# A decoder layer on one core: the gates' weight sums made in place on VectorE, and the down projections' sums read from scratch

## The chip, the cores and the metric

The kernel runs on one core of a Trainium2 chip. The metric is device time in microseconds. Three timed runs of the kernel before gave a median of 2127.15 us (2127.11 to 2127.19).

## The reference

One layer of a hybrid decoder, for 16 learned and 256 given positions (only the 256 are returned), model width 2048. All arrays are float32.

```python
u = rms_norm(h, g1);  h = h + 0.5 * (silu(u @ w_gate) * (u @ w_up)) @ w_down      # first FFN, width 5632
u = rms_norm(h, g2);  z = u @ w_in                                               # q k v, indexer, conv, two gates
y_attn = sparse_attention(q, k, v, indexer top 64) @ w_attn_branch
y_conv = (b * causal_conv3(c * xc)) @ w_conv_branch
merged = sigmoid(ga) * y_attn + sigmoid(gc) * y_conv
h = h + merged @ w_out
u = rms_norm(h, g3);  h = h + 0.5 * (silu(u @ w2_gate) * (u @ w2_up)) @ w2_down  # second FFN
```

## The kernel before

TensorE multiplies in float32r, which keeps only part of a float32 number. So every weight block is split on the chip into a rounded part (whi, ScalarE, L250) and the rest (wlo, VectorE, L251), and one product is three matmuls: activation-high by whi, activation-high by wlo, activation-low by whi (L641 to L643, and L430 to L432 in the earlier stages).

The program is one stream of weights. `Stream.loads` lists the transfers, in order, into a ring in on-chip memory of 12 slots of 128x512 elements; `Stream.subs` lists the units that are split, at most 1024 columns each. SyncE's queue issues the loads (L216), and a load is issued when the units that had its slots are split. A unit is split into one of four buffers of whi and wlo, and three units ahead of the one that TensorE works on (`AHEAD`). Each call of `Stream.next` that opens a unit issues, in this order, the steps due early, the split three units on, the loads that then fit, and the steps due late. So the order of each engine's instructions is fixed when the program is built.

The stages in order of time: first FFN (to about 800 us), input projections with the attention, the convolution (to 1090), the gates with the two branch products (1090 to 1343), the output projection, the second FFN (from 1434).

In the gates and in the second FFN the products go by pairs: two blocks of 128 input rows by two blocks of 512 columns. A plain pair (kind "C") takes eight products with 128 tokens each and four weight blocks in two units. The others save one product, as in Winograd's form of Strassen's method: seven products, with seven weight blocks, four of which are sums or differences of the weights (the signs lie in the token side), in four units of 2, 2, 2 and 1 blocks. The seven results are put together afterwards on VectorE (`recombine`, L720 to L723). Two ways of making the weight sums exist:

- Kind "P": `Stream.prepare` does it long ahead. GpSimd's queue fetches the 1 MB of four blocks (L178), VectorE makes four adds of 512 columns (L182), GpSimd's queue stores the result to a scratch tensor in DRAM (L185), and the stream later loads it from there. Most of these run in the first FFN; `LATE` says how many run in the input projections and how many beside the convolution. The 15 seven-product pairs of the gates (3 in the first group of 512 columns, 4 in each of the other three) and the 52 of the second FFN's gate and up projections are of this kind.
- Kind "D", in the down projections of the second FFN: shortly before use, one load on SyncE's queue (L163) and one accumulating transfer on GpSimd's queue (L164) make two of the sums, and VectorE the other two (L228, L229).

The down projection runs in three parts, over four, four and three groups of 512 hidden columns, each in two halves of 1024 output columns. A half of a long part has eight pairs, three of kind D; a half of the short part has six, two of kind D. The token side's sums for them are made in `turn_mid`.

A group of gates has eight pairs, then 8 units of branch weights, multiplied with the attention's and the convolution's results (`pbr`), then `merge` (six VectorE steps, L1242 and L1244), which is issued at the start of the next group.

## Time and profile before

| what | value |
|---|---|
| time, median of three runs | 2127.15 us |
| the profiled execution's own time | 2127.65 us |
| its span, first to last instruction | 2125.8 us |
| TensorE busy | 2109.4 us |
| VectorE busy | 1638.3 us |
| ScalarE busy | 1125.2 us |
| granted TensorE clock | 1.000 |

Rows of instructions give line, engine, operation, output and inputs, shapes and a count, then busy time and the mean of one in ns, then the idle time before them and what ended it. A row of the timeline begins with its start and its length in us, and ends in brackets with the idle time of the engine before it and what ended that. Waits give in total, times, longest. Rows by stage give, per engine, busy us and the number of instructions, then the granted clock, the DMA engines' share and GB/s. PE is TensorE's matmuls, PEld its weight loads, DVE VectorE, ACT ScalarE, POOL GpSimd, SP SyncE; q behind one is its queue. In rows of transfers the last number is the median time from issue to landing.

### The profile page before, as it was taken

The numbers are of one execution on the slowest core, as the hardware profiler recorded it, in microseconds if no ns is written. First come the engines' busy times: TensorE is split into PE (matmuls) and PEld (weight loads), VectorE is DVE, ScalarE is ACT, GpSimd is POOL, SyncE is SP. The second block draws the span as 40 slices with busy tenths as digits, with TensorE's granted clock in tenths as the row PEclk, the third lists the DMA queues.
The fourth block names the chain that finished last, engine by engine and source line by source line (L and its number), as shares of the span: only waits on it lengthen the run. The fifth ranks groups of instructions, "written<-read, shape, count | busy, mean of one in ns | idle before, by whom it ended". The sixth has DMA issues, their size and how long they took to land.

```text
span 2125.8 us, 33282 instructions
## 1 busy us (share of the span) xinstructions
PE 2109.4 (99%) x12973; PEld 1902.1 (89%) x12973; DVE 1638.3 (77%) x2150; ACT 1125.2 (53%) x1455; POOL 122.8 (6%) x196
## 2 busy tenths in 40 slices
PE   8999999999999999999999999999999999999999
PEld 8999999999999999888988888888888888888887
DVE  7777766677777766788777777687898889888887
ACT  5444433344444445555455566467675566656664
POOL 2000000000000110000000000010000000000000
PEclk9999999999999999999999999999999999999999
DMA  7798899988999967855577777567888888789884
GB/s 284 289 349 337 335 352 338 357 338 336 350 343 350 341 220 272 306 199 211 219 262 240 246 268 252 177 211 249 301 320 269 259 318 316 259 256 302 304 273 149
DMA packets 126302, 603.60 MB, mean 284 GB/s; under 512 B 14048, under 2 KB 14176, under 8 KB 85312
## 3 DMA queue, kind: packets, MB, share of 16 engines
q1 hardware_dynamic: 104256, 451.98, 59.7%
q0 software_dynamic: 21744, 149.33, 19.8%
q8 instruction: 101, 1.65, 0.3%
q14 instruction: 57, 0.47, 0.1%
q10 hardware_dynamic: 144, 0.17, 0.0%
HBM read 529.07 MB, written 72.35 MB: 283 GB/s over the span
## 4 chain that ended last, share of the span: by engine, by line
PE 96%; DVE 2%; ACT 1%; DMA 1%; POOL 0%; issue 0%; SPq 0%; DVEq 0%
PE q L641 13%; PE q L642 13%; PE q L643 13%; PE pd L430 4%; PE pd L432 4%; PE pd L431 4%; PE pu L432 4%; PE pg L432 4%; PE pg L431 4%; PE pu L431 4%; PE pg L430 4%; PE pu L430 4%; PE po L445 3%; PE po L447 1%; PE pbr L641 1%; PE pbr L643 1%
## 5 line engine op out<-in xcount | busy, mean ns | idle before, releaser
L251 DVE TENSOR_TENSOR wlo<-raw,whi 128x1024 fp32r<-128x1024 f32 (+1 forms) x887 | 1018.8, 1165 | 437.2 <-ACT whi L250 423.6
L250 ACT ACTIVATE whi<-raw 128x1024 fp32r<-128x1024 f32 (+1 forms) x887 | 888.0, 1011 | 881.6 <-PE q L643 220.2
L641 PE MATMUL q<-whi,act 128*128 128x512 f32 x713 | 278.8, 391 | 0.0
L643 PE MATMUL q<-whi,act 128*128 128x512 f32 x713 | 277.6, 389 | 0.0
L642 PE MATMUL q<-wlo,act 128*128 128x512 f32 x713 | 277.5, 389 | 0.0
L430 PE MATMUL pd<-mid,whi 128*128 128x272 f32 x704 | 201.8, 287 | 0.0
L432 PE MATMUL pd<-mid,wlo 128*128 128x272 f32 x704 | 201.8, 287 | 0.0
L431 PE MATMUL pd<-mid,whi 128*128 128x272 f32 x704 | 201.8, 287 | 0.0
L430 PE MATMUL pg<-act,whi 128*128 128x272 f32 x672 | 192.8, 287 | 0.0
L432 PE MATMUL pg<-act,wlo 128*128 128x272 f32 x672 | 192.6, 287 | 0.0
L431 PE MATMUL pg<-act,whi 128*128 128x272 f32 x672 | 192.6, 287 | 0.0
L430 PE MATMUL pu<-act,whi 128*128 128x272 f32 x672 | 192.6, 287 | 0.0
L432 PE MATMUL pu<-act,wlo 128*128 128x272 f32 x672 | 192.6, 287 | 0.0
L431 PE MATMUL pu<-act,whi 128*128 128x272 f32 x672 | 192.6, 287 | 0.0
L182 DVE TENSOR_TENSOR prep<-prep 128x512 f32<-128x512 f32 x268 | 183.2, 684 | 9.8 <-DMA prep<-in_w2p_dram 9.4
L643 PEld LDWEIGHTS q<-whi,act 128*128 128x128 f32 x713 | 133.9, 188 | 27.9
L642 PEld LDWEIGHTS q<-wlo,act 128*128 128x128 f32 x713 | 133.9, 188 | 27.2
L641 PEld LDWEIGHTS q<-whi,act 128*128 128x128 f32 x713 | 133.9, 188 | 27.2
L430 PEld LDWEIGHTS pd<-mid,whi 128*128 128x128 f32 x704 | 132.6, 188 | 0.0
L431 PEld LDWEIGHTS pd<-mid,whi 128*128 128x128 f32 x704 | 132.6, 188 | 0.0
L432 PEld LDWEIGHTS pd<-mid,wlo 128*128 128x128 f32 x704 | 132.6, 188 | 0.0
L431 PEld LDWEIGHTS pg<-act,whi 128*128 128x128 f32 x672 | 126.6, 188 | 0.0
(281 smaller groups left out, 3859.6 us busy)
## 6 DMA issues: line engine op xcount, KB each, us to landing
raw<-in_wgu_dram SPq DMA_DIRECT2D x87, 1024.0 KB, 7.2
raw<-in_w_dram SPq DMA_DIRECT2D x128, 512.0 KB, 5.7
prep<-in_w2p_dram POOLq DMA_DIRECT2D x52, 1024.0 KB, 9.0
s<-prep POOLq DMA_DIRECT2D x52, 1024.0 KB, 6.1
raw<-s SPq DMA_DIRECT2D x104, 512.0 KB, 5.9
raw<-in_wd_dram SPq DMA_DIRECT2D x44, 1024.0 KB, 6.7
raw<-in_w2p_dram SPq DMA_DIRECT2D x52, 512.0 KB, 6.2
raw<-in_wcv_dram SPq DMA_DIRECT2D x24, 1024.0 KB, 4.8
```

The source lines that it names most:

```text
L182: nc.vector.tensor_add(x[out], x[a], x[b])
L250: nc.scalar.activation(to[0], raw, AF.Copy)
L251: nc.vector.tensor_sub(to[1], raw, to[0].bitcast(F32))
L430: nc.tensor.matmul(ps, whi, xhi, start=first, stop=False)
L431: nc.tensor.matmul(ps, whi, xlo, start=False, stop=False)
L432: nc.tensor.matmul(ps, wlo, xhi, start=False, stop=last)
L445: nc.tensor.matmul(ps.rearrange("p (a t) -> p a t", a=2), whi, x(i), start=i == 0, stop=False)
L447: nc.tensor.matmul(ps[:, :SEQ], wlo, x(i)[:, 0, :], start=False, stop=i == total - 1)
L641: nc.tensor.matmul(ps, xhi, whi, start=n == 0, stop=False)
L642: nc.tensor.matmul(ps, xhi, wlo, start=False, stop=False)
L643: nc.tensor.matmul(ps, xlo, whi, start=False, stop=n == total - 1)
```

## The change

1. The gates' 15 seven-product pairs become kind "Q". Nothing is prepared for them: the raw weights of a pair are loaded into the ring, and `sum_ahead` makes the four sums on VectorE in the ring's own slots, at the step before the one that splits the pair's first unit. The number and size of the stream's loads there stay, and so do their places in the ring.
2. Kind "D" is gone, with its accumulating transfers. The down projections' seven-product pairs are of kind "P", and a half of a long part has four of them in place of three; a half of the short part keeps two.
3. So 72 pairs are prepared in place of 67. `LATE` moves one from beside the convolution to the input projections, and the steps of those beside the convolution start eight units later.
4. In the second FFN the ring grows by six slots in place of two; the room is that of the tiles that D used.
5. In the last half the last two results are finished one after the other (`apart`), where before their products alternated.
6. The token sums for `turn_mid` have a fourth place, and are made one step later.

```diff
-LATE = (7, 5)
+SUMS = ((1, 1, 0), (0, 0, 2), (2, 2, 1), (3, 3, 2))
+LATE = (8, 4)
...
-    return list(zip("CCCPPPCC", [0, 2, 4, 3, 5, 7, 6, 1]) if c == 0 else zip("CPPCPPCC", [0, 3, 5, 2, 7, 1, 4, 6]))
+    return list(zip("CCCQQQCC", [0, 2, 4, 3, 5, 7, 6, 1]) if c == 0 else zip("CQQCQQCC", [0, 3, 5, 2, 7, 1, 4, 6]))
...
-            ("CCDCDCDC", [(0, 2), (1, 2), (0, 0), (2, 2), (1, 0), (3, 0), (2, 0), (3, 2)]),
-            ("CDCDCDCC", [(0, 2), (0, 0), (1, 2), (1, 0), (2, 2), (2, 0), (3, 0), (3, 2)]),
+            ("CCPPCPPC", [(0, 2), (1, 2), (0, 0), (1, 0), (2, 2), (2, 0), (3, 0), (3, 2)]),
+            ("CPPCPPCC", [(0, 2), (0, 0), (1, 0), (1, 2), (2, 0), (3, 0), (2, 2), (3, 2)]),
...
-        self.loads += [(src[:, 2 * WIDE : 4 * WIDE], 2 * WIDE), (src[:, 4 * WIDE :], WIDE)]
-        self.added[g] = len(self.doubles)
-        self.doubles.append((g, src))
-        self.subs += [(g, "sa", 0, 2, WIDE), (g, "sb", 0, 2, WIDE), (g, "raw", 0, 2, WIDE), (g + 1, "raw", 0, 1, WIDE)]
+        src = ahead.pop(0)
+        g = len(self.subs)
+        self.add(src, 4, WIDE, False)
+        self.add(src[:, WIDE:], 3, WIDE, False)
+        self.subs[g] = (self.subs[g][0], "sums") + self.subs[g][2:]
...
-        self.ring += [(raw, i) for i in range(2)]
+        self.ring += [(raw, i) for i in range(6)]
...
         for g, kind, _, _, _ in self.subs[self.n_split : self.n_split + 2]:
-            if kind == "sa" and self.sum_pool and g not in self.summed:
+            if kind == "sums" and g not in self.summed:
                 self.load(g + 2)
                 self.summed.add(g)
-                one, last = self.raw[g], self.raw[g + 1]
-                sb = self.sum_pool.tile([P, 2 * WIDE], F32, name="sb", tag="sb")
-                add(sb[:, :WIDE], self.sums[g, "sa"][:, WIDE:], one[:, :WIDE])
-                add(sb[:, WIDE:], sb[:, :WIDE], last[:, :WIDE])
-                self.sums[g, "sb"] = sb
+                x = [self.raw[g + j // 2][:, j % 2 * WIDE : (j % 2 + 1) * WIDE] for j in range(4)]
+                for out, a, b in SUMS:
+                    self.nc.vector.tensor_add(x[out], x[a], x[b])
...
+        if apart:
+            w = [st.next(), st.next()]
+            for c, xs in ((c1, (b21, b11)), (c2, (b22, b12))):
+                for x, block in zip(xs, w):
+                    mac3(c, x, block)
+            return
...
-        st.prepare(lambda i: mp.tile([P, RAW], F32, name="prep", tag="tA"), LATE[1], 1, units2 + 6, units2 + 46)
+        st.prepare(lambda i: mp.tile([P, RAW], F32, name="prep", tag="tA"), LATE[1], 1, units2 + 14, units2 + 47)
```

Two places on VectorE show how the instructions move. The first is the third group of gates, from the end of `merge` on. `wlo<-raw,whi` is the split of a unit (1024 or 512 columns); before:

```order
L1244 TENSOR_TENSOR vm_13276<-va,vx 128x512
L1244 TENSOR_TENSOR vm_13277<-vv,ve 128x512
L251 TENSOR_TENSOR wlo<-raw,whi 128x1024 x2
L251 TENSOR_TENSOR wlo<-raw,whi 128x512
L251 TENSOR_TENSOR wlo<-raw,whi 128x1024 x3
L251 TENSOR_TENSOR wlo<-raw,whi 128x512
L251 TENSOR_TENSOR wlo<-raw,whi 128x1024 x5
L251 TENSOR_TENSOR wlo<-raw,whi 128x512
```

And now, where `raw<-raw` x4 is one in-place sum of a Q pair:

```order
L1220 TENSOR_TENSOR vm_12859<-va,vx 128x512
L1220 TENSOR_TENSOR vm_12860<-vv,ve 128x512
L228 TENSOR_TENSOR wlo<-raw,whi 128x1024 x2
L212 TENSOR_TENSOR raw<-raw 128x512 x4
L228 TENSOR_TENSOR wlo<-raw,whi 128x512
L228 TENSOR_TENSOR wlo<-raw,whi 128x1024 x3
L228 TENSOR_TENSOR wlo<-raw,whi 128x512
L228 TENSOR_TENSOR wlo<-raw,whi 128x1024
L212 TENSOR_TENSOR raw<-raw 128x512 x4
L228 TENSOR_TENSOR wlo<-raw,whi 128x1024 x4
L212 TENSOR_TENSOR raw<-raw 128x512 x4
L228 TENSOR_TENSOR wlo<-raw,whi 128x512
```

The second pair's sum stands ahead of the first pair's last unit; the third's stands ahead of the second unit of the plain pair between; the fourth's ahead of the third pair's last unit. The rest of the order is as before.

The second place is beside the convolution, where the attention's softmax begins (`soft`, `mx`, `sm`); `prep<-prep` is an add of a prepared pair. Before:

```order
L1152 SCALAR_TENSOR_TENSOR cy<-cx,small,cy 128x256 x2
L182 TENSOR_TENSOR prep<-prep 128x512
L251 TENSOR_TENSOR wlo<-raw,whi 128x1024
L453 TENSOR_TENSOR t<-pb,u 128x256
L1160 TENSOR_TENSOR cy<-t,cy 128x256
L467 TENSOR_TENSOR cs_10039<-cy,cs_10039 128x256
L1023 SCALAR_TENSOR_TENSOR soft<-psc,acc_8834 128x576
L1029 TENSOR_REDUCE mx<-soft 128x4
L1023 SCALAR_TENSOR_TENSOR soft<-psc,acc_8835 128x544
L1029 TENSOR_REDUCE mx<-soft 128x2
L182 TENSOR_TENSOR prep<-prep 128x512
L251 TENSOR_TENSOR wlo<-raw,whi 128x1024
```

And now:

```order
L1128 SCALAR_TENSOR_TENSOR cy<-cx,small,cy 128x256 x2
L228 TENSOR_TENSOR wlo<-raw,whi 128x1024
L425 TENSOR_TENSOR t<-pb,u 128x256
L1136 TENSOR_TENSOR cy<-t,cy 128x256
L439 TENSOR_TENSOR cs_10086<-cy,cs_10086 128x256
L999 SCALAR_TENSOR_TENSOR soft<-psc,acc_8874 128x576
L1005 TENSOR_REDUCE mx<-soft 128x4
L999 SCALAR_TENSOR_TENSOR soft<-psc,acc_8875 128x544
L1005 TENSOR_REDUCE mx<-soft 128x2
L228 TENSOR_TENSOR wlo<-raw,whi 128x1024
```

The first pair's adds are gone from this stretch, and the four pairs that stay come later.

## The prediction

> **What bounds the kernel now.** I read the page's head, the waits of TensorE, busy time by stage, and then the gates stage on the timeline.

> ```profile
> span 2125.8 us, 33282 instructions
> PE 2109.4 (99%) x12973; PEld 1902.1 (89%) x12973; DVE 1638.3 (77%) x2150; ACT 1125.2 (53%) x1455; POOL 122.8 (6%) x196
> PE start L430 <- ACT whi L250: 7.0, 1, 7.0
> PE psc L1017 <- DVE soft L1023: 1.0, 1, 1.0
> PE pcg L432 <- DVE wlo L251: 0.9, 2, 0.6
> PE q L641 <- DVE vx L1359: 0.7, 1, 0.7
> PE pqt L921 <- DVE zz L824: 0.3, 1, 0.3
> ...
> core 0: us, PE busy (x) PEld busy (x) DVE busy (x) ACT busy (x) POOL busy (x), PEclk, DMA share, GB/s
> 39.00:800.00 761.00, 761.00 (x6170) 760.81 (x6168) 540.35 (x715) 314.91 (x380) 66.85 (x119) 1.00 0.87 328
> 930.00:1090.00 160.00, 157.86 (x1129) 145.41 (x1128) 123.28 (x204) 82.17 (x159) 13.43 (x18) 1.00 0.61 218
> 1090.00:1343.00 253.00, 252.49 (x1123) 208.17 (x1122) 183.04 (x201) 146.88 (x168) 0.00 (x0) 1.00 0.73 247
> 1434.00:2100.00 666.00, 665.05 (x2993) 550.42 (x2992) 576.88 (x667) 427.86 (x498) 14.03 (x16) 1.00 0.84 283
> ```

> TensorE works 2109.4 of 2125.8 us, and what it waits between start and tail is under 4 us. So a gain can only come from fewer matmuls, and a loss from any place where VectorE stops keeping ahead. In the gates stage (1090 to 1343) VectorE has 183.0 us of work in 253, which looks like 70 us of room; in the second FFN (1434 to 2100) it is at 87% and TensorE still never starves. The question is whether the room in the gates lies where the new work falls.

> **The matmuls removed.** Each of the four long down halves turns one plain pair (eight products) into a seven-product pair: 4 products, 12 matmuls.

> ```profile
> 1199.78 0.39 PE L641 MATMUL pbr<-whi,ys 128*128 128x512 f32 x1
> ...
> 1200.46 0.39 PE L641 MATMUL pbr<-whi,cs 128*128 128x512 f32 x1
> ```

> Three starts in 0.68 us: a product costs 0.68, not three times the 0.39 that one record shows. So **-2.7 us**.

> **The second FFN's accumulating transfers.** GpSimd's sixteen leave, with two sums each on VectorE.

> ```profile
> L228 DVE TENSOR_TENSOR sb<-sd,raw 128x512 f32<-128x512 f32 x16 | 10.9, 682 | 0.0
> L229 DVE TENSOR_TENSOR sb<-sb,raw 128x512 f32<-128x512 f32 x16 | 11.1, 692 | 0.6
> sd<-in_w2d_dram POOLq DMA_DIRECT2D x16, 512.0 KB, 8.1
> ```

> 22 us of VectorE work and 8.1 us landings go, but TensorE waited only 0.7 us there (L1359), so at most that comes back; the other way, each of the four exchanged pairs is split in four units instead of two, well under the 22 us. I take 0 (-0.7 to +1). The ring, four slots larger than before in this stage, can hide more, but nothing is exposed.

> **The prepared sums.** 67 pairs were summed ahead, now 72: 60 instead of 55 in the first FFN, 8 instead of 7 in the projections, 4 instead of 5 beside the convolution.

> ```profile
> L182 DVE TENSOR_TENSOR prep<-prep 128x512 f32<-128x512 f32 x268 | 183.2, 684 | 9.8 <-DMA prep<-in_w2p_dram 9.4 <-DMA prep<-in_wgp_dram 0.3
> prep<-in_w2p_dram POOLq DMA_DIRECT2D x52, 1024.0 KB, 9.0
> s<-prep POOLq DMA_DIRECT2D x52, 1024.0 KB, 6.1
> 966.57 0.69 DVE L182 TENSOR_TENSOR prep<-prep 128x512 f32<-128x512 f32 x1
> ```

> In the first FFN that is 20 more adds (20 x 0.684 = 14 us, into 221 us of idle) and 10 more transfers of 1 MB on GpSimd's queue, 10.5 MB beside the 250 MB (761 us at 328 GB/s) that keep the DMA engines at 0.87: they go to about 0.91. I take 0 (0 to +2). Beside the convolution the pair taken away is the first, whose adds stood among the softmax steps; the wait of psc and one of pcg follow directly behind the one at 966.57. I take **-0.9** (-2 to 0).

> **The tail.**

> ```profile
> 2119.26 3.73 SPq L1402 DMA_DIRECT2D out_dram<-ht  x4
> 2121.26 1.37 DVE L1399 SCALAR_TENSOR_TENSOR ht<-q,ht 128x512 f32<-128x512 f32 x2 [1.35 <-PE q L643]
> ```

> The last half's last tile still ends with the last matmul; the tile before it is now finished one product (0.68) earlier, so two output transfers overlap less. **-0.3** (-0.7 to 0).

> **The gates: 15 in-place sums.** Each is four adds of 512 columns on one piece of the ring, each reading what the one before wrote. The nearest rows, a dependent add behind another and then an unrelated split:

> ```profile
> 1598.09 0.68 DVE L228 TENSOR_TENSOR sb<-sd,raw 128x512 f32<-128x512 f32 x1
> 1598.80 0.69 DVE L229 TENSOR_TENSOR sb<-sb,raw 128x512 f32<-128x512 f32 x1
> 1599.41 1.22 DVE L251 TENSOR_TENSOR wlo<-raw,whi 128x1024 fp32r<-128x1024 f32 x1
> ```

> A dependent add starts 0.71 after the one before, an unrelated instruction 0.61 after: a sum is 3 x 0.71 + 0.61 = 2.74 us. [...]

> Now the third group of gates (C Q Q C Q Q C C). I call a, b, c, d the four units of a seven-product pair (two weight blocks each, d one) and a, b the two of a C pair.

> ```profile
> 1215.42 0.39 PE L641 MATMUL q<-whi,act 128*128 128x512 f32 x1
> ...
> 1215.13 0.68 DVE L1242 TENSOR_TENSOR va<-pbr,va 128x512 f32<-128x512 f32 x1
> ...
> 1218.73 2.35 DVE L251 TENSOR_TENSOR wlo<-raw,whi 128x1024 fp32r<-128x1024 f32 x2
> 1221.72 0.69 DVE L251 TENSOR_TENSOR wlo<-raw,whi 128x512 fp32r<-128x512 f32 x1 [0.64 <-ACT whi L250]
> ...
> 1221.06 0.63 ACT L250 ACTIVATE whi<-raw 128x512 fp32r<-128x512 f32 x1 [1.66 <-PE q L643]
> ...
> 1228.76 1.06 ACT L250 ACTIVATE whi<-raw 128x1024 fp32r<-128x1024 f32 x1 [0.52 <-DMA raw<-in_wg_dram]
> 1230.01 1.07 ACT L250 ACTIVATE whi<-raw 128x1024 fp32r<-128x1024 f32 x1 [0.18 <-DMA raw<-sg]
> 1232.09 1.06 ACT L250 ACTIVATE whi<-raw 128x1024 fp32r<-128x1024 f32 x1 [1.01 <-DMA raw<-sg]
> ...
> 1224.77 1.69 SPq L216 DMA_DIRECT2D raw<-sg  x2
> ...
> raw<-in_wb_dram SPq DMA_DIRECT2D x32, 512.0 KB, 6.3
> raw<-sg SPq DMA_DIRECT2D x26, 512.0 KB, 4.7
> ```

> Three things stand in it. A unit costs VectorE 1.13 (2.35 for two, the last shown 1.22), a half one 0.61; so a Q pair is 3 x 1.13 + 0.61 + 2.74 = 6.7 us of VectorE for 7 x 0.68 = 4.76 of TensorE. ScalarE's rounding waits for TensorE to release one of four buffers ("<-PE q"), so splits run at most three units ahead: 4 us of a Q pair; VectorE cannot use its idle time of the branch products for later pairs. And the ring is already at its limit: the last rounding above (Q3a and Q3b are the two "sg" waits) waited 1.01 for a load issued by 1226.46 and landed at 1232.09, 5.6 us later. Its slot came free with the split of Q2b, and the sum of the third Q pair needs that same load, but stands one unit earlier on VectorE, with the split of Cb queued behind it and TensorE waiting for Cb.

> With the clock at 0 at 1215.42: the merge and Q1b, Q1c end at 5.7 as now. Sum 2 ends at 8.4, Q1d at 9.0, Q2a (rounded after its sum, 1.06) at 10.7. TensorE comes to Q2a at 10.2 and can do one matmul without the low part: it stops 0.3. Q2b is split at 11.9, Ca at 14.8. Sum 3 needs Q3b's load, issued at 12.0, landed at 17.4 (5.4 us, between the stage's median of 4.7 and this place's 5.6): it ends at 19.5, Cb's split at 20.7. TensorE wanted that at 18.2: **2.5**. Q3c is split at 24.1; sum 4 needs the load into Cb's slot, issued at 20.8 and landed at 25.5, ends at 27.6 and Q3d at 28.2, against 27.4: **0.8**. Q4a at 29.9 against 28.9: **1.0**. Behind that come the two C pairs, 10.9 us of TensorE for 4.5 of splits, and the backlog is gone. Together 4.6 us, in three groups 13.8. The first group (C C C Q Q Q C C) has no C between, but the token sums of one pair (1.7 us) fall in: the same reckoning stops at Q2c 0.3, Q2d 2.7 and Q3a 0.9, together 4. The gates: **+17.8 us**.

> Bounds: with every load there in time only work counts. VectorE then needs, from the merge through Q4a, 3.3 + 11 x 1.13 + 3 x 0.61 + 3 x 2.74 = 25.8 us and twice 0.5 where it waits for the rounding behind a sum: 26.8, against 5.44 + 4.76 + 4.76 + 5.44 + 4.76 + 0.23 = 25.4 at which TensorE wants it. [...] With landings of 7 us (the slowest kind of this stage, the branch weights, has 6.3 in the median), sum 3 and sum 4 move by 1.6 and 2.3: 8.5 a group, some 30 in all.

> **The sum.** -2.7 + 0 - 0.9 - 0.3 + 17.8 = +13.9. The profiled execution took 2127.65 (span 2125.8 and 1.85 around it), 0.5 over the median of 2127.15 that the result is held against: 2127.15 + 13.9 = **2141.0**.

> **The rivals.** *The cover holds* (the other side): if loads land as now and VectorE's few late splits are absorbed by the three units ahead, the gates cost nothing and -3.9 is left, with L1359's wait -4.6: 2122.6 to 2123.3. For it: 70 us of idle, and TensorE needs a unit's low part one matmul late. Against: 6.7 for 4.76, twice in a row. It decides where the four adds of a sum take under about 1.0 us, or splits run further ahead; neither has a row. Chance 0.09. *Work only*: the loads are not late, since the stalls themselves space them; the gates cost 4 to 8, less 3.9: 2127 to 2131. For it: the median landing of 4.7; against: the waits at 1228.76 to 1232.09, which are there already without any sum. Chance 0.13. *The loads chase the splits*: each late split frees its slot late and so makes the next load late, up to the +30 above: 2153 and more. Chance 0.07. *The first FFN's transfers*: at 0.91 the ring's 1 MB loads come late and add up to 5; chance 0.05, on top of the others. That the change does not do what it says is hardly possible here (the products and the sums can be counted in the order): 0.01, at 2127.

> **How the numbers follow.** The forecast, with 2.5 to 6.5 us a group, has 0.70 and lies at 2134 to 2150. A measurement of this kernel tells about 0.2% (4.3 us) from no change. Faster than 2122.9: half of the cover case and some slack, 0.06. Within 0.2%: the other half and nearly all of the work-only case, 0.15. Slower: 0.79. The range leaves out the cover case and the worst of the chase: 2128 to 2152.

> **What would show it.** Right: in the profile after, TensorE waits for VectorE's wlo on q lines, 10 to 25 us in all, all between 1090 and 1360, at the units named; VectorE waits for loads of the gate weights inside the in-place sums; the last stage is 2.7 us of TensorE shorter. Wrong in the price: the waits are there but a sum is 2.4, or the loads land within 4. Wrong in kind: no TensorE waits in the gates, or new ones in the first FFN for whi of L227 behind a load, or in the second FFN.

## The result, and the profile after

| kernel | median | runs | ratio to the kernel before |
|---|---|---|---|
| before | 2127.17 us | 2127.11 to 2127.68, 4 runs | |
| after | 2141.33 us | 2138.84 to 2142.07, 4 runs | 1.0064, 95% interval 1.0051 to 1.0077 |

The change makes the kernel 14.2 us slower; 13.9 was forecast, and the time lies inside the forecast range. The profiled execution took 2142.07 us, its span is 2140.3.

The page's head, TensorE's waits that come to over a microsecond once the kernel is under way, and the busy time of three stages, over the same stretches as before:

```profile
span 2140.3 us, 33445 instructions
PE 2113.4 (99%) x12961; PEld 1904.6 (89%) x12961; DVE 1676.7 (78%) x2214; ACT 1132.9 (53%) x1469; POOL 114.8 (5%) x190
```

```profile
PE q L614 <- DVE wlo L228: 11.7, 6, 3.4
PE pbr L613 <- DVE ms L439: 1.4, 2, 1.2
```

```profile
39.00:800.00 761.00, 761.00 (x6170) 760.86 (x6169) 552.74 (x735) 314.98 (x380) 72.37 (x129) 1.00 0.90 342
1090.00:1343.00 253.00, 239.82 (x1033) 195.14 (x1032) 209.78 (x252) 136.12 (x157) 0.00 (x0) 0.97 0.70 230
1434.00:2100.00 666.00, 666.00 (x3029) 553.93 (x3028) 570.08 (x657) 440.04 (x525) 2.01 (x2) 1.00 0.82 287
```

The first FFN is as full as it was (761.00 of 761, the DMA engines at 0.90 in place of 0.87). The second FFN has no wait left. Everything lost lies in the gates: in the same 253 us, 1033 matmuls ran where there were 1123. VectorE has 26.7 us more work in them and is still 43 us idle, and the granted clock, 1.00 before, is 0.97. The stage runs from its first matmul to the output projection's first; before, then after:

```profile
1088.10 0.40 PE L641 MATMUL q<-whi,act 128*128 128x512 f32 x1
1343.36 1.52 PE L445 MATMUL po<-ms,whi 128*128 128x512 f32 x6
```

```profile
1087.10 0.40 PE L613 MATMUL q<-whi,act 128*128 128x512 f32 x1
1362.92 1.30 PE L417 MATMUL po<-ms,whi 128*128 128x512 f32 x5
```

The stage took 255.26 and now 275.82 us: +20.56. It starts 1.0 us earlier, and what follows it is shorter: 2125.8 - 1343.36 = 782.44 before, 2140.3 - 1362.92 = 777.38 after, -5.06. Together +14.5, as the spans say (2140.3 - 2125.8).

Where the 20.56 arise is seen in the third group, whose clock 0 is at 1224.41 here. VectorE from the second sum on:

```profile
1230.05 2.87 DVE L212 TENSOR_TENSOR raw<-raw 128x512 f32<-128x512 f32 x4
1232.83 5.83 DVE L228 TENSOR_TENSOR wlo<-raw,whi 128x512 fp32r<-128x512 f32 x6
1241.21 0.69 DVE L212 TENSOR_TENSOR raw<-raw 128x512 f32<-128x512 f32 x1 [2.56 <-DMA raw<-in_wgq_dram]
1242.54 2.14 DVE L212 TENSOR_TENSOR raw<-raw 128x512 f32<-128x512 f32 x3 [0.64 <-DMA raw<-in_wgq_dram]
1244.60 4.62 DVE L228 TENSOR_TENSOR wlo<-raw,whi 128x1024 fp32r<-128x1024 f32 x4
```

Sum 2 runs at once. Sum 3 cannot: VectorE has split all that its order puts ahead of it by 1238.6 and stands 2.56 us until the first load of the third Q pair has landed, and 0.64 until the second has. The split of Cb, whose weights are long there, is queued behind. Over the whole stage these waits of VectorE for loads come to 9.4 us:

```profile
DVE raw L212 <- DMA raw<-in_wgq_dram: 9.4, 6, 2.6
```

TensorE's side of it:

```profile
1242.11 0.39 PE L613 MATMUL q<-whi,act 128*128 128x512 f32 x1
1245.88 0.50 PE L614 MATMUL q<-wlo,act 128*128 128x512 f32 x1 [3.38 <-DVE wlo L228]
1246.21 0.39 PE L615 MATMUL q<-whi,act 128*128 128x512 f32 x1
...
1247.01 0.63 PE L615 MATMUL q<-whi,act 128*128 128x512 f32 x1
1247.44 0.63 PE L613 MATMUL q<-whi,act 128*128 128x512 f32 x1
1247.87 0.63 PE L614 MATMUL q<-wlo,act 128*128 128x512 f32 x1
...
1250.00 0.48 PE L613 MATMUL q<-whi,made 128*128 128x512 f32 x1
1250.32 0.40 PE L614 MATMUL q<-wlo,made 128*128 128x512 f32 x1
```

One matmul with Cb's high part goes, then 3.38 us of nothing. And some 4.5 us after the stop began, matmuls start 0.43 us apart in place of 0.227, with no wait named: from 1246.21 to 1250.32 eleven starts take 4.11 us where 11 x 0.227 = 2.50 would do, so 1.6 us more. The rows by time say what that is: the granted clock falls from 1.00 to 0.50 for 3.41 us.

```profile
1243.35:1246.77 3.42, 0.89 (x4) 0.77 (x5) 3.39 (x4) 2.97 (x3) 0.00 (x0) 1.00 0.25 100
1246.77:1250.18 3.41, 3.41 (x10) 2.62 (x9) 3.38 (x5) 0.10 (x1) 0.00 (x0) 0.50 0.77 219
1250.18:1253.59 3.41, 3.41 (x17) 2.78 (x16) 3.13 (x5) 2.18 (x3) 0.00 (x0) 1.00 0.87 299
```

The other groups have one such stop each: 2.32 us at the second matmul of Q2d in the first, 3.27 and 2.34 at Cb in the second and fourth, and after each the same slow stretch. With the longer steps around them the four stops come to 12.0 us, the four slow stretches to about 6.6; 0.95 is a longer wait for the merged results at the last branch product.

### The profile page after: what moved, and what is told of

Its sections match the earlier page's. It is cut to its first block, busy times and chain, and to the rows that moved or that the text cites. A ratio compares the mean times of both kernels' runs of the same rounds, so it can differ in the third digit from the quotient of the medians.

```text
span 2140.3 us, 33445 instructions
## 1 busy us (share of the span) xinstructions
PE 2113.4 (99%) x12961; PEld 1904.6 (89%) x12961; DVE 1676.7 (78%) x2214; ACT 1132.9 (53%) x1469; POOL 114.8 (5%) x190
## 4 chain that ended last, share of the span: by engine, by line
PE 92%; DVE 4%; DMA 2%; ACT 1%; issue 1%; POOL 0%; SPq 0%; ACTq 0%; DVEq 0%
PE q L614 12%; PE q L615 12%; PE q L613 12%; PE pd L402 4%; PE pd L403 4%; PE pd L404 4%; PE pg L404 4%; PE pu L404 4%; PE pg L402 4%; PE pu L402 4%; PE pg L403 4%; PE pu L403 4%; PE po L417 3%; DVE wlo L228 2%; PE po L419 1%; PE pbr L613 1%
## 5 line engine op out<-in xcount | busy, mean ns | idle before, releaser
L227 ACT ACTIVATE whi<-raw 128x1024 fp32r<-128x1024 f32 (+2 forms) x927 | 926.9, 1011 | 903.1 <-PE q L615 264.3
L228 DVE TENSOR_TENSOR wlo<-raw,whi 128x1024 fp32r<-128x1024 f32 (+2 forms) x927 | 1060.5, 1164 | 396.7 <-ACT whi L227 385.5
L167 DVE TENSOR_TENSOR prep<-prep 128x512 f32<-128x512 f32 x288 | 196.9, 684 | 15.7 <-DMA prep<-in_w2p_dram 15.5
L615 PEld LDWEIGHTS q<-whi,act 128*128 128x128 f32 x713 | 134.7, 189 | 28.2
## 6 DMA issues: line engine op xcount, KB each, us to landing
raw<-in_wgu_dram SPq DMA_DIRECT2D x87, 1024.0 KB, 6.5
prep<-in_w2p_dram POOLq DMA_DIRECT2D x72, 1024.0 KB, 9.1
sums<-prep POOLq DMA_DIRECT2D x72, 1024.0 KB, 5.7
raw<-sums SPq DMA_DIRECT2D x144, 512.0 KB, 5.7
raw<-in_w_dram SPq DMA_DIRECT2D x120, 512.0 KB, 6.4
raw<-in_wd_dram SPq DMA_DIRECT2D x44, 1024.0 KB, 8.1
raw<-in_w2p_dram SPq DMA_DIRECT2D x72, 512.0 KB, 5.7
raw<-in_wcv_dram SPq DMA_DIRECT2D x24, 1024.0 KB, 4.8
```

What stands on the lines that cost most here:

```text
L167: nc.vector.tensor_add(x[out], x[a], x[b])
L227: nc.scalar.activation(to[0], raw, AF.Copy)
L228: nc.vector.tensor_sub(to[1], raw, to[0].bitcast(F32))
L615: nc.tensor.matmul(ps, xlo, whi, start=False, stop=n == total - 1)
```

## The experiments

Each is an edit of the kernel after, except the two clock runs, which edit the kernel before; "..." in a diff stands for lines left out, among them those that give a tile or a scratch tensor its room. Two theories stood against each other: **loads** (a sum waits for a load that the full ring issues too late, and holds up splits behind it) and **work** (VectorE has too much to do in a row: 6.7 us for 4.76 of TensorE, twice). The kernel before was run again beside them. Its median was 2127.53 us beside the first three below and the one with the gates prepared as before, 2127.52 beside the two that rearrange the first group and the longer clock run, and 2127.36 beside the other four.

**Without the sums.** The four adds are left out.

```diff
-                for out, a, b in SUMS:
+                for out, a, b in ():
```

> The changed kernel without the gates' in-place adds (the sums of the gates' weights are left out, so those products are of raw blocks; all loads and splits stay). Both theories on the sums: the gates stage goes back to its length before, 20.5 us less: 2121, 2119 to 2123. Rival, that the loads from the input in place of the scratch tensor, or the larger number of prepared pairs, cost part of it: above 2125.

2121.76 us (ratio 0.9971, 0.9960 to 0.9982). TensorE has no q wait left, and the gates take 255.4 us (first q matmul to 1342.53, the first of the output projection) as in the kernel before. So the sums are the whole loss, and the rest of the change is worth 5.8 us.

**The same adds on another tile.** VectorE adds as often and as long, but on a tile that no load writes, so nothing waits for a load and the products use the plain weights.

```diff
-                x = [self.raw[g + j // 2][:, j % 2 * WIDE : (j % 2 + 1) * WIDE] for j in range(4)]
+                x = [self.spare[:, j % 2 * WIDE : (j % 2 + 1) * WIDE] for j in range(4)]
...
+        st.spare = gp.tile([P, 2 * WIDE], F32, name="spare")
...
```

> The changed kernel with the same sixty adds at the same places on VectorE, but on a tile of their own that no load writes (the gates' weight sums are left out; the ring's blocks are used raw). The work stays, the wait for loads goes. The load: the third pair's adds run at once, Cb's split is then 0.2 late instead of 3.4, so groups two to four lose their 5.2 us each; the first group, where no load was waited for, keeps its 2.3 us and the slow matmuls: 2141.3 - 16 = 2125, 2123 to 2129. The work: all four groups keep their waits, 2139 to 2141.

2131.26 us (1.0026, 1.0006 to 1.0045): between the two, and outside both forecasts. Of the loss against the run without sums, 19.6 us, 9.5 stay here and 10 go with the wait for loads. TensorE's waits on q fall to 2.9 us, of which the first group's stop is 2.3; there no load was late in the kernel after either. But its waits for merged results at the branch products are 3.5 us, where the kernel after has 1.4 and the run with two more slots, below, 0.5. Why is open, so the 9.5 are no clean price of the work. (The profiled execution took 2151.6 us, and the gates began 20.5 us later in it than in the kernel after; it is read for the gates alone.)

**The sum one step later.** A sum behind a plain pair is made behind that pair's second unit, so that Cb's split is ahead of it.

```diff
-            if kind == "sums" and g not in self.summed:
+            if kind == "sums" and g not in self.summed and (g == self.subs[self.n_split][0] or self.subs[self.n_split][4:] == (WIDE,) and self.subs[self.n_split][3] == 1):
```

> The changed kernel with one step moved: a sum that follows a plain pair is made behind the split of that pair's second unit, not ahead of it (one place in each of groups two to four; the sum of each group's first pair moves too, where nothing waits). Theory, the load: the third pair's sum waits on VectorE for a load whose slot came free late, and the plain unit's split that TensorE needs is queued behind it. Then the 2.3 to 3.4 us waits at that unit go, waits of 0.8 and 1.5 us come later (third pair's first and last unit), too short for the slow matmuls that followed the long waits: about 2.6 us a group less, 2141.3 - 8 = 2133, 2131 to 2137. Rival, the work: VectorE simply has too much to do in that stretch; the order of the same work does not matter, 2141.

2140.18 us (1.0055, 1.0040 to 1.0070): in the median 1.2 us under the kernel after, and not the 8 of the load theory. The profiled execution is the shortest of the four, 2136.76 us with a granted clock of 1.000; the others took 2139.82 to 2141.02 at 0.999. In it the stop at Cb is gone, but it is paid in pieces:

```profile
PE q L614 <- DVE wlo L228: 9.1, 16, 2.3
```

```profile
DVE raw L212 <- DMA raw<-in_wgq_dram: 3.3, 3, 1.5
```

Sixteen waits in place of six, 9.1 us in place of 11.7: VectorE waits less for loads (9.4 before), but the sum stands in front of its own pair's splits. Moving the sum only moves the stop; no slow matmuls follow it in this execution. The run does not separate the theories as I had meant it to.

**Two more slots.** The ring gets 1024 more columns in the gates alone, from room that is free there. No instruction of VectorE or TensorE changes its place.

```diff
         room.append(gp)
+        wider = gp.tile([P, SUB], F32, name="raw")
+        st.ring += [(wider, i) for i in range(2)]
...
+        st.ring = st.ring[:12]
+        st.pos = st.pos if st.pos < 12 else 0
         tags = ("q2", "q3", "q4", "q8", "q1", "q5", "q6", "q7")
```

> Two more 512-column slots of the ring during the gates, so that the load which the third sum waits for can be issued about one unit of TensorE time earlier. Load theory: the waits of 3.3 and 3.4 us at Cb fall towards the 2.3 of the group without a late load, the waits of VectorE for loads inside the sums (9.4 us) halve, and the kernel lands at 2134 to 2138. Work theory: the loads are a symptom, the stall stays where VectorE's own work puts it, and the time stays at 2140 to 2142.

2129.77 us (1.0008, 0.9999 to 1.0017): 11.6 us come back, more than expected. VectorE's waits for loads, 9.4 us in the kernel after, are:

```profile
DVE raw L212 <- DMA raw<-in_wgq_dram: 1.0, 2, 0.6
```

and in the third group, the place shown above, sum 3 follows the splits without a gap, and the stop at Cb is gone:

```profile
1225.96 2.87 DVE L212 TENSOR_TENSOR raw<-raw 128x512 f32<-128x512 f32 x4
1228.75 5.83 DVE L228 TENSOR_TENSOR wlo<-raw,whi 128x512 fp32r<-128x512 f32 x6
1234.49 2.87 DVE L212 TENSOR_TENSOR raw<-raw 128x512 f32<-128x512 f32 x4
1237.28 4.62 DVE L228 TENSOR_TENSOR wlo<-raw,whi 128x1024 fp32r<-128x1024 f32 x4
```

VectorE's instructions and their order are the same, and so is its work, 220.2 us over the whole stage against 220.9. This decides it for the loads in the last three groups. What stays is the first group's 2.33 and 1.13 in the fourth.

**Every second pair prepared.** In the gates no two in-place sums stand side by side (8 sums in place, 7 pairs prepared).

```diff
-    return list(zip("CCCQQQCC", [0, 2, 4, 3, 5, 7, 6, 1]) if c == 0 else zip("CQQCQQCC", [0, 3, 5, 2, 7, 1, 4, 6]))
+    return list(zip("CCCQPQCC", [0, 2, 4, 3, 5, 7, 6, 1]) if c == 0 else zip("CQPCQPCC", [0, 3, 5, 2, 7, 1, 4, 6]))
...
-LATE = (8, 4)
+LATE = (10, 5)
...
```

> The down halves as changed; in the gates every second of the seven-product pairs is prepared again (8 sums in place, 7 prepared), so that no two in-place sums stand side by side; 79 prepared pairs, 64 of them in the first FFN, 10 in the projections, 5 beside the convolution. If the loss comes from the adjacency (a second sum before VectorE has caught up, and its load) the gates fall to within 0 to 3 us of the kernel before, and the whole is 2121 to 2125, faster than both. If each in-place sum costs its own stall, the gates lose about half of what they lost, 8 to 10 us: 2130 to 2132. If 64 prepared pairs are already too many for the transfers of the first FFN (75 were), TensorE waits there and it is over 2125 whatever the gates do.

2142.38 us (1.0069, 1.0056 to 1.0081). My guess that the side-by-side sums do it was wrong, and the loss is not halved either, as it would be if each sum cost a stall of its own. The third group again (of the shortest of five executions, 2139.68 us), with the pair ahead of the plain one prepared:

```profile
1238.36 1.23 DVE L228 TENSOR_TENSOR wlo<-raw,whi 128x1024 fp32r<-128x1024 f32 x1 [0.22 <-ACT whi L227]
1239.51 0.68 DVE L212 TENSOR_TENSOR raw<-raw 128x512 f32<-128x512 f32 x1
1242.18 2.15 DVE L212 TENSOR_TENSOR raw<-raw 128x512 f32<-128x512 f32 x3 [1.99 <-DMA raw<-in_wgq_dram]
```

VectorE had caught up (it waits for ScalarE's rounding in the first row) and still stands 1.99 us in the sum for the pair's second load. One sum alone is enough: it needs two loads a unit sooner than a split would, and by the run with two more slots it is the ring that issues them too late; this arrangement itself was not run with more slots. Beside that the five pairs beside the convolution now end in the gates: one of their fetches landed late, VectorE stood 7.6 us for it, and TensorE has five waits of 0.3 to 0.9 us in the first group.

**Gates prepared as before, down halves as now.** 87 prepared pairs, 75 of them in the first FFN.

```diff
-    return list(zip("CCCQQQCC", [0, 2, 4, 3, 5, 7, 6, 1]) if c == 0 else zip("CQQCQQCC", [0, 3, 5, 2, 7, 1, 4, 6]))
+    return list(zip("CCCPPPCC", [0, 2, 4, 3, 5, 7, 6, 1]) if c == 0 else zip("CPPCPPCC", [0, 3, 5, 2, 7, 1, 4, 6]))
...
```

> The first part undone alone: the gates' 15 pairs prepared ahead again, the down projections as changed, so 87 prepared pairs, 75 of them in the first FFN. If the gates' sums are the whole loss and the first FFN carries 15 more prepared pairs (41 us of VectorE work into 208 us of idle, 31 MB more on DMA engines at 0.90): 2141.3 - 20.5 = 2121, under both kernels. Rival, the first FFN's transfers: DMA goes to 0.98 there, the ring's loads come late and TensorE waits 5 us or more: 2126 and above.

2162.16 us (1.0146, 1.0122 to 1.0171). The gates are full, and the first FFN is not:

```profile
39.00:800.00 761.00, 733.25 (x5820) 730.18 (x5819) 551.59 (x762) 296.44 (x354) 82.54 (x151) 0.98 0.95 370
1090.00:1343.00 253.00, 253.00 (x1240) 213.85 (x1238) 184.95 (x212) 141.63 (x162) 4.26 (x6) 1.00 0.75 250
```

```profile
DVE prep L167 <- DMA prep<-in_w2p_dram: 161.5, 46, 10.2
ACT whi L227 <- DMA raw<-in_wgu_dram: 58.3, 25, 4.8
```

With the DMA engines at 0.95 the fetches of the pairs land late, and VectorE, in order, stands 161.5 us before adds whose data is not there (8.4 us in the kernel after, at 0.90); the splits behind them wait. TensorE stands idle for 27.8 us of the 761, and with the slow matmuls behind its stops the gates begin 43.3 us later than in the kernel after (1130.37 against 1087.10). With 64 pairs, the run above, TensorE still had all of its 761 us:

```profile
39.00:800.00 761.00, 761.00 (x6170) 760.92 (x6169) 560.65 (x751) 316.01 (x380) 77.68 (x137) 1.00 0.92 353
```

**Three of eight.** The long down halves with three prepared pairs, as many as before.

```diff
-            ("CCPPCPPC", [(0, 2), (1, 2), (0, 0), (1, 0), (2, 2), (2, 0), (3, 0), (3, 2)]),
-            ("CPPCPPCC", [(0, 2), (0, 0), (1, 0), (1, 2), (2, 0), (3, 0), (2, 2), (3, 2)]),
+            ("CCPCPCPC", [(0, 2), (1, 2), (0, 0), (2, 2), (1, 0), (3, 0), (2, 0), (3, 2)]),
+            ("CPCPCPCC", [(0, 2), (0, 0), (1, 2), (1, 0), (2, 2), (2, 0), (3, 0), (3, 2)]),
```

> The long down halves go back to three prepared pairs of eight (60 prepared pairs in place of 72, 48 of them in the first FFN); the gates keep their in-place sums. The term for the removed matmuls says +2.7 us over the changed kernel: about 2144. If the twelve extra prepared pairs cost something in the first FFN that the trace does not show, it comes back here and the time stays at 2141 or falls; if the split of a seven-product pair in four units costs VectorE anything in the second FFN, the difference is under 2.

2143.65 us (1.0074, 1.0059 to 1.0090), 2.3 over the kernel after. The traces give it without the gates: from the output projection's first matmul to the end it is 780.1 us here and 777.4 in the kernel after, so 2.7 for the four products, as forecast. The kernel before has the same products as this run, and 782.4 (781.6 and 782.0 in the two clock runs below, which share its second FFN). So taking away the accumulating transfers, with the larger ring, was worth 1.5 to 2.4 us by itself.

**The clock by itself.** The kernel before, with the last add of each of the first three merges repeated, so that TensorE stops in each of the groups and nothing else is changed; first 5, 6 and 7 times, then 8, 9 and 10.

```diff
-                    nc.vector.tensor_add(m[j], box[a], box[b])
+                    for _ in range((5, 6, 7, 1)[c] if j else 1):
+                        nc.vector.tensor_add(m[j], box[a], box[b])
```

> The kernel before, with the last add of each gate group's merge repeated 5, 6 and 7 times in the first three groups, so that TensorE stops once in each by some 1.5, 2.1 and 2.8 us, and nothing else changes. If a single stop of a certain length is what halves the clock some 4 us later, matmul starts of 0.43 us in place of 0.227 follow the longest stop, perhaps the middle one, and not the shortest, at about 2 us each; together 2127 + 6.4 + 2 to 4 = 2135 to 2138. If the slow starts belong to the in-place sums (VectorE's adds or the loads) and not to the stop, no matmul slows down and it is 2127 + 6.4 = 2133 to 2134.

> As the run with 5, 6 and 7 adds, with 8, 9 and 10: the kernel before with single stops of some 2.4, 3.2 and 3.9 us and no in-place sums. If a stop of over 2 us is what halves the clock, slow starts of 0.43 us follow the last two and perhaps the first, 2 us each: 2127.4 + 10.5 + 4 to 6 = 2142 to 2144. If they belong to the in-place sums, there are none: 2137 to 2138.

2132.24 us (1.0021, 1.0012 to 1.0030) and 2143.52 us (1.0074, 1.0060 to 1.0088). In the first, stops of 0.30, 1.03 and 1.75 us and not one slow matmul; they were some 1.1 us shorter than meant, hence the second run. In the second, stops of 2.48, 3.20 and 3.93, and slow starts behind all three. The longest stop of each:

```profile
1291.09 0.50 PE L642 MATMUL q<-wlo,made 128*128 128x512 f32 x1 [1.75 <-DVE wlo L251]
1291.43 0.39 PE L643 MATMUL q<-whi,made 128*128 128x512 f32 x1
```

```profile
1299.21 0.79 PE L642 MATMUL q<-wlo,made 128*128 128x512 f32 x1 [3.93 <-DVE wlo L251]
1299.80 0.63 PE L643 MATMUL q<-whi,made 128*128 128x512 f32 x1
1300.23 0.63 PE L641 MATMUL q<-whi,act 128*128 128x512 f32 x1
...
1304.49 0.56 PE L642 MATMUL q<-wlo,act 128*128 128x512 f32 x1
1304.89 0.39 PE L643 MATMUL q<-whi,act 128*128 128x512 f32 x1
```

There are no in-place sums here and no late loads, so the slow matmuls belong to the stop.

**More ring, and the first group rearranged.** Two slots with the first group as C C Q Q C Q C C; and three slots with C C C Q C Q C C, which gives up one seven-product pair (0.68 us). The edit of the second, against the run with two more slots:

```diff
-        wider = gp.tile([P, SUB], F32, name="raw")
-        st.ring += [(wider, i) for i in range(2)]
+        wider = gp.tile([P, 3 * WIDE], F32, name="raw")
+        st.ring += [(wider, i) for i in range(3)]
...
-    return list(zip("CCCQQQCC", [0, 2, 4, 3, 5, 7, 6, 1])
+    return list(zip("CCCQCQCC", [0, 2, 4, 3, 6, 5, 7, 1])
```

> Two more slots of the ring in the gates, and in the first group the three in-place sums no longer side by side (C C Q Q C Q C C). The first group's stop of 2.3 us came from three sums and three pairs' token sums in a row on VectorE; if so it goes, with the slow matmuls behind it: 2129.8 less 2.6 to 4.9, so 2125 to 2127, below the kernel before. If the token sums, which the first of the three now needs two units earlier, are late instead, the stop only moves and it stays at 2128 to 2130.

> Three more slots in place of two, and the first group with two seven-product pairs apart from each other in place of three in a row (C C C Q C Q C C), which adds one product (0.68 us). If the load is all that is left of the fourth group's stop (1.13 us) and the row of sums all of the first group's, both go: 2129.8 - 1.1 - 4.2 + 0.7 = 2125, faster than the kernel before by 0.1%. If a sum costs TensorE something even with its load there, 2127 to 2129.

2129.53 us (1.0010, 1.0001 to 1.0019): the first group's stop only moved (0.65 for the token sums and 1.50 some ten microseconds on, no slow matmuls), as its second theory had it. And **2124.95 us** (0.9989, 0.9980 to 0.9998): below both kernels, with no stop left at a gate product. TensorE's longest waits, those at the start of the kernel aside:

```profile
PE pcg L404 <- DVE wlo L228: 0.9, 2, 0.6
PE pbr L613 <- DVE ms L439: 0.5, 2, 0.3
```

The third slot took the fourth group's 1.13, since nothing else differs there. The margin to the kernel before, 2.6 us, is small: the interval ends at 0.9998. Against the run without sums 3.2 us are left. The product given up is 0.7 of it; 2.4 are two matmul steps of about 0.51 in place of 0.23 in each of the last three groups, with the step behind each 0.11 longer, to which the profile gives no releaser. With the loads in time, the work of 14 sums costs TensorE no more than these 2.4.

## Why the prediction was right, and where it was not

The total was right (+13.9, measured +14.2) by a mechanism that held, and its closeness is luck. In the profiled executions the gates cost 2.8 us more than forecast (20.56 against 17.8), and what lies around them gained 2.2 more (6.1 against 3.9). Within the gates, too, 6.6 us of slow matmuls that the sum did not have stand in the place of 6.3 us of later stops that did not come.

- **Matmuls, -2.7.** Held: 2.7 by the traces of the run with three of eight.
- **Second FFN's accumulating transfers, 0 (-0.7 to +1).** Mis-sized: what follows the gates became 5.06 us shorter, and the products explain 2.7 of it. The other 2.4 are there in the run with three of eight as well, whose three passages through down projections are 0.5, 1.2 and 0.5 us shorter than those of the kernel before. There the two sums (L228, L229) had stood right ahead of steps that TensorE waited for; that the sums did it, and not the smaller ring, was not tested. Looking only at the wait that the profile named, 0.7, was the mistake.
- **Tail, -0.3.** Nothing came of it: from the end of the last matmul to the end of the span it is 3.94 us before and 3.91 after.
- **Prepared sums, 0 in the first FFN, -0.9 beside the convolution.** Held: 761.00 of 761, and the gates start 1.0 earlier. What went is the wait of psc (1.0). The forecast put one of pcg's two waits behind the same add; both stand ahead of it, at 948 and 954 us, and stayed. The rival of late transfers in the first FFN is real, but only beyond this change: TensorE lost nothing to it with 64 pairs there, and 27.8 us of idle time with 75.
- **A sum, 2.74 us.** Held: 1230.05 to 1232.83 is 2.78.
- **Cb's stop, 2.5 a group, from a late load.** The mechanism held, place and cause: the second add of sum 3 stood at clock 18.1 (forecast 17.4), and the stops are 3.27, 3.38 and 2.34. The ring run shows the cause.
- **Q2a 0.3, Q3d 0.8, Q4a 1.0.** Failed. I let the rounding of a pair's first unit wait for the whole sum; it needs only the two blocks that the first two adds write. After the sum that begins at 1230.05 ScalarE rounds at once behind the second add:

```profile
1231.63 1.06 ACT L227 ACTIVATE whi<-raw 128x1024 fp32r<-128x1024 f32 x1 [0.94 <-DVE raw L212]
```

  VectorE also had the time to catch up while TensorE ran at a granted clock of 0.50.
- **The clock, not in the sum at all.** Missed: about 1.6 to 1.8 us behind each stop. It stands by chance where I had 2.1 us of later stops.
- **First group, 4.** Half held: stops of 0.24 at Q2c and 2.32 at Q2d, from work and token sums, where 0.3 and 2.7 were forecast; at Q3a 0.17 in place of 0.9, for the same reason as in the other groups. The slow matmuls behind them bring it to 4 by chance.

Of the rivals, *work only* is what is left when the loads are in time: it said 2127 to 2131, and the runs with other data and with two slots gave 2131.3 and 2129.8. The 8 of its 4 to 8 us is 3 x (26.8 - 25.4) and the first group's 4; the lower 4 was my estimate for sums of about 2.4 us, and no run shows such a sum: it took 2.78 here. *The loads chase the splits* did not happen: the last three groups grew alike. *The cover holds* fails at 12 slots; at 15, with one sum fewer, it nearly does (2124.95, where 2122.6 to 2123.3 was named).

## What to carry to other kernels

An operation that an in-order engine does in place on a prefetch buffer moves the deadline of that buffer's load forward, to the operation and ahead of all that is queued behind it. Before adding one, find the load's issue, its landing and the slot that it needs; idle time of the engine (70 us here) says nothing about it, and one more slot or two can be worth more than any reordering: 11.6 us here for 4 KB a partition, where moving the sum gained about 1. In the gates here every stop of TensorE from 2.48 us up, and five of nine between 1.9 and 2.4, had slow matmuls behind it (last section); such a stop is to be priced with them, some 1.7 us each time in the kernel after.

## What the hardware showed

The length of the stop alone does not decide it. Two stops of 2.33 us, the first from the run with three of eight, the second from that with every second pair prepared:

```profile
1115.74 0.50 PE L614 MATMUL q<-wlo,act 128*128 128x512 f32 x1 [2.33 <-DVE wlo L228]
...
1117.47 0.63 PE L615 MATMUL q<-whi,made 128*128 128x512 f32 x1
1117.90 0.63 PE L613 MATMUL q<-whi,made 128*128 128x512 f32 x1
1118.32 0.63 PE L614 MATMUL q<-wlo,made 128*128 128x512 f32 x1
```

```profile
1121.38 0.50 PE L616 MATMUL q<-wlo,act 128*128 128x512 f32 x1 [2.33 <-DVE wlo L228]
...
1123.10 0.39 PE L615 MATMUL q<-whi,made 128*128 128x512 f32 x1
1123.32 0.39 PE L616 MATMUL q<-wlo,made 128*128 128x512 f32 x1
1123.56 0.39 PE L617 MATMUL q<-whi,made 128*128 128x512 f32 x1
```

Behind the first the matmuls start 0.43 us apart, behind the second 0.22 to 0.24. What makes the difference was not tested. By its clocks one kernel was hit in some executions and spared in others: 3.41 us at 0.50 are an estimated 0.0008 of the mean clock over 2128 us, and in the ten executions with two more slots the granted clock was 0.999 in seven, of 2129.62 to 2130.23 us, and 1.000 in three, of 2128.22 to 2129.28.

The DMA engines in the first FFN: at a busy share of 0.92 (every second pair prepared) TensorE was busy for 761.00 of 761 us; at 0.95 (all prepared) it stood idle for 27.8 us.
